# Value weights in their own buffers, and six weight residues made by accumulating DMAs, in a two-layer decoder trunk in float32

## The chip, the core and the metric

The kernel runs on one core of a Trainium2 chip. A core has a matrix engine (TensorE; the profile calls its matmuls PE and its weight loads PEld), a vector engine (VectorE, DVE), a scalar engine (ScalarE, ACT), a general engine (GpSimd, POOL) and an engine that mostly issues transfers (SyncE, SP). Transfers (DMAs) are issued on queues of SP, ACT and POOL; each engine works through its own list of instructions in order. The metric is the device time of one execution in microseconds.

## The reference

The input is one sequence of 256 tokens of width 1024. All weights and all arithmetic are float32.

```
h = x
hn = rms_norm(h, g[0,0])
h += stick_breaking_attention(hn, w_qkv, w_o)           # 16 heads of 64
h += (relu(rms_norm(h, g[0,1]) @ w1[0])**2) @ w2[0]     # 1024 -> 4096 -> 1024
shared = nsa_shared_kv(h, kv_norm, ...)                 # keys and values, compressed blocks
hn = rms_norm(h, g[1,0])
h += nsa_attention(hn, w_q, gate_b, w_o, shared)        # compressed, selected and window branch, gated
h += (relu(rms_norm(h, g[1,1]) @ w1[1])**2) @ w2[1]
out = rms_norm(h, final_norm)
```

In `stick_breaking_attention` the product `hn @ w_qkv` gives queries, keys and values. The kernel makes the values first.

## The kernel before

**Number format.** Matmuls run on the type fp32r, a float32 rounded to fewer bits. To keep float32's precision, each operand is split into a high part (a cast to fp32r, `wh` for weights) and a low part (what the cast lost, `wl = raw - wh`). A product is then made of three matmuls: high by high, high by low and low by high.

**The weight stream.** All weights come as one list of pieces (`stream`), most of 128 partitions by 2048 columns (1 MB), in the order of their use: the values' weights `wv` first, then `wqk`, `wo0`, the first MLP's `w1` and `w2` (alternating: `w1` piece c, then `w2` piece c-2), and so on. `fetch` (L252 to L265) issues the load of the next piece on SP into one of three buffers `raw`. `split` (L276 to L307) makes the two parts, half a piece at a time: the cast on ACT (L293), the subtraction on DVE (L299). After the second half's subtraction it calls `fetch` for the next piece, so a load waits until a buffer is read out. The parts lie in three buffers each (`wh`, `wl`, `NB = 3`); a piece can be split once TensorE is done with the piece three before it.

**The order of the work.** TensorE's instructions are in the order of the program. What ACT, DVE and POOL do, and in which order, is decided while the program is written out, by a planner (`Order`): it keeps a clock, a cost formula for each operation, a rank for each chain of operations and an expected landing time for each load (`ws.landed`), and gives each engine, when free, the ready operation of the lowest rank. Its choice is then fixed; at run time an engine that waits holds up all that stands behind it.

**The start** (`layer0`, from L555). Eight warming matmuls run until data come. The values `pv` are made from x, transposed, in blocks of 128 of its 1024 columns (k = 0 to 7). `load` brings the blocks of x (`xraw`; the first on ACT's queue, the others on SP's), `turned` splits a block into `xa` high (L568 on ACT or L569 on DVE) and low (L571). `v_first` computes block 0 with the first two weight pieces of 256 KB, `v_proj` the others with pieces cut by `V_CUT`: five of one block (512 KB) and one of two (1 MB). The residual stream `hres` and constants are loaded behind them, then the eight pieces `wqk`; `proj` makes queries and keys (`qk`). A broadcast of the norm's factor (`pr`) stands between values and queries.

**The first MLP** (`mlp`). For each of 16 column blocks c, `first` multiplies the activations by `w1` piece c (`pu`: for each half of 128 output columns, eight wide matmuls with the high weights, then eight narrow ones with the low weights), then `second` multiplies the squared result of block c-2 by a `w2` piece (`acc`).

**The end** (`finish`). For each token tile the squares are summed on ACT (L1431), the sum is closed on DVE (L1434), its power -0.5 is taken on POOL (L1436), the residual stream is multiplied by the gain on DVE (L1425), and the rows are scaled on ACT (L1418, 384 columns) and on DVE (L1420, two pieces of 320 columns); each scaled piece is stored at once (L1421).

Of the kernel before, what the change touches and what calls it, by code (L numbers as in the profile page):

```python
# [8 lines left out]
F32 = mybir.dt.float32  # L9
# [3 lines left out]
OP = mybir.AluOpType  # L13
AX = mybir.AxisListType

P = 128
D = 1024
T = 2
NK = D // P
NH = 16  # L20
DH = 64
# [3 lines left out]
DFF = 4096  # L25
NFC = 16
NGN = 6
V_CUT = ((1, 1), (2, 1), (3, 1), (4, 1), (5, 1), (6, 2))
EPS = 1e-5
NEG = -1e30  # L30
GELU_C = 2.0 * 0.7978845608028654
# [1 line left out]
C_CAP, C_ANY, C_COS, C_SIN, C_BLK, C_PW, C_ROT, C_ROS, C_CMT, C_CB, C_END = (  # L33
    0, 384, 386, 418, 450, 458, 462, 718, 974, 1230, 1486)
# [124 lines left out]
def act(n, f, more=0):  # L159
    return {"A": (195 + 0.835 * n + more, f, False)}  # L160
# [6 lines left out]
def pool(n, f, more=0):  # L167
    return {"G": (185 + 1.67 * n + more, f, True)}
# [3 lines left out]
def hybrid_kernel(ctx, tc, x, xt, eye, gcols, gfin, wqk, wv, wo0, wkv, wvs, wq, wg, wo1, w1, w2, cw1, cw2, cpos, gate_b, consts, out):  # L172
    nc = tc.nc

    cp = ctx.enter_context(tc.tile_pool(name="cp", bufs=1))
    wp = ctx.enter_context(tc.tile_pool(name="wp", bufs=3))
# [4 lines left out]
    o = Order()  # L181

    def go(gen, rank=1, lag=LAG):
        return Chain(o, gen, rank, o.now + lag)
# [6 lines left out]
    def slot(i, shape, dt, name):  # L191
        return cp.tile(shape, dt, tag=f"e{i}", name=name, bufs=1)
# [49 lines left out]
    i_m.append(feed_mlp(1))  # L242

    class Weights:
        raws, made, parts, gone, cur, landed = [], [], [], 0, -1, 0.0

    ws = Weights()
    ways = {"hi": "A"}

    def fetch():  # L250
        j = len(ws.raws)
        if j == len(stream):  # L252
            return
        src, n, whole = stream[j]
        raw = wp.tile([P, n], F32, tag="raw", name="raw", bufs=3)
        ws.raws.append(raw)
        ws.made.append(None)
        cuts = 2 if j == 0 else 1
        for c in range(cuts):
            r = slice(c * n // cuts, (c + 1) * n // cuts)  # L260
            nc.sync.dma_start(raw[:, r], src[:, r])
        for h in range(2):
            if h < cuts:
                ws.landed = max(o.t + 1900, ws.landed) + P * n * 4 / cuts / 330
            ws.parts.append(Chain(o, whole_part(j, h) if whole else split(j, h), rank_of(j), ws.landed))  # L265

    def rank_of(j):
# [7 lines left out]
    def split(j, half):  # L275
        n = stream[j][1]  # L276
        if 2 * j + half:
            yield ws.his[2 * j + half - 1]
        before = [i for i in range(j) if not stream[i][2]]
        while len(before) >= NB and ws.gone <= before[-NB]:  # L280
            w = Waiter()
            ws.waiting.append(w)
            yield w
        ws.parts[2 * j + half].rank = rank_of(j)
        r = slice(half * n // 2, (half + 1) * n // 2)

        def hi(e):
            def f():
                if ws.made[j] is None:
                    ws.made[j] = (wp.tile([P, n], F32R, tag="wh", name="wh", bufs=NB),  # L290
                                  wp.tile([P, n], F32R, tag="wl", name="wl", bufs=NB))
                if e == "A":
                    nc.scalar.copy(ws.made[j][0][:, r], ws.raws[j][:, r])  # L293
                else:
                    nc.vector.tensor_copy(ws.made[j][0][:, r], ws.raws[j][:, r])
            return f

        def lo():
            nc.vector.tensor_sub(ws.made[j][1][:, r], ws.raws[j][:, r], f32(ws.made[j][0][:, r]))  # L299

        m = n // 2
        k = {"A": (195 + 0.835 * m, hi("A"), False), "D": (200 + 0.49 * m, hi("D"), True)}
        yield {e: k[e] for e in ways["hi"]}
        ws.his[2 * j + half].finish()
        yield {"D": (150 + 1.045 * m, lo, True)}
        if half:
            fetch()  # L307

    class Waiter(Chain):
# [76 lines left out]
    def rstd_of(t, rs):  # L386
        v = []
        yield from variance(t, v)
        r = sp.tile([P, 1], F32, name="r", bufs=4)
        yield pool(1, lambda: nc.gpsimd.tensor_tensor(r, v[0], npow, op=OP.pow), 370)  # L390
        rs[t] = r
# [162 lines left out]
    def layer0(ap):  # L554
# [3 lines left out]
            mm(warm, nc.const_aps.tensor(1.0, [P, P], BF16), nc.const_aps.tensor(1.0, [P, 512], BF16), True, True)  # L558
        xn = x_tiles(0, "a")
        v = slot(0, [P, T, D], F32, "v0")  # L560
        xg = slot(1, [P, NK + NK * T * P], F32, "xraw")
        xraw = xg[:, NK:].rearrange("p (k q) -> p k q", k=NK)
        pv = [[B(2 * n + t, f"pv{t}{n}") for n in range(2)] for t in range(T)]
        in_x = [None] * NK

# [6 lines left out]
                xn[1][:, k, :], xraw[:, k, :], g, f32(xn[0][:, k, :]), op0=OP.mult, op1=OP.subtract), port=True)  # L572

        def load(k0, k1):
            a, b = NK * (k0 > 0) + k0 * T * P, NK + k1 * T * P
            (nc.sync if k0 else nc.scalar).dma_start(xg[:, a:b], xt[:, a:b])
            ws.landed = max(o.t + 1900, ws.landed) + P * (k1 - k0) * 1024 / 330
            for k in range(k0, k1):
                in_x[k] = Chain(o, turned(k), 0.4, ws.landed)

# [13 lines left out]
        def v_proj(i):  # L594
            k0, m = V_CUT[i]
            for kk in range(m):
                k = k0 + kk
                o.need(in_x[k])
                for n in range(2):
                    w = W(i_v[i], n if m == 1 else kk)  # L600
                    c = cut(w, kk * D + n * 512, kk * D + (n + 1) * 512)
                    for a, b in ((0, 0), (1, 0), (0, 1)):
                        for t in range(T):
                            mm(pv[t][n], tok(xn, k, t)[a], c[b], False, k == NK - 1 and b == 1)
            gone(i_v[i])
# [2 lines left out]
        o.run(o.now)  # L608
        load(0, 1)
        fetch()  # L610
        fetch()
        load(1, 2)
        fetch()
        load(2, 4)
        nc.scalar.dma_start(gc, gcols)
        go_on = ap.tile([P, 2 * ROW], BF16, name="go_on", bufs=1)
        nc.gpsimd.memset(go_on, 1.0)
        nc.gpsimd.memset(go_on.rearrange("p (h c) -> p h c", h=2)[:, :, 2 * SEG - 1:ROW:SEG], 0.0)
        v_first(0)
        v_first(1)  # L620
        load(4, 8)
        v_proj(0)
        v_proj(1)
        for t in range(T):
            nc.sync.dma_start(hres[t], x[t * P:(t + 1) * P, :])
        nc.sync.dma_start(ident, eye)
        nc.sync.dma_start(cst[:, 0:C_ROT], consts[:, 0:C_ROT])
        ws.landed = max(o.t + 1900, ws.landed) + 4500
        rstd = [None, None]
        rc = [Chain(o, rstd_of(t, rstd), 1.5, ws.landed) for t in range(T)]  # L630
        v_proj(2)
        v_proj(3)
        v_proj(4)
        v_proj(5)
        o.need(*rc)
        rbq = ap.tile([P, 2, T * P], F32, name="rbq", bufs=1)
        pr = B(6, "pr")
# [762 lines left out]
    nc.sync.dma_start(gf, gfin.to_broadcast([P, D]))  # L1400
    ssq = [sp.tile([P, 4], F32, name=f"ssq{t}", bufs=1) for t in range(T)]
    ys = [slot(1 + t, [P, 2, D], F32, f"ys{t}") for t in range(T)]
    last, gained = [[], []], [[], []]
    ends = [[(0, 512)]] * 3 + [[(0, 256), (256, 512)]]

    def finish(i, q, c):
        t, n = divmod(i, 2)
        k = len(last[t])
        end = i % 2 == 1 and q[1] == 512
        q = slice(n * 512 + q[0], n * 512 + q[1])  # L1410
        m = q.stop - q.start
        ss, sq, y = ssq[t], ys[t][:, 0, :], ys[t][:, 1, :]
        part = ss[:, 3:4]

        def scaled(e, a, b):
            def f():
                if e == "A":
                    nc.scalar.activation(y[:, a:b], y[:, a:b], AF.Copy, scale=part)  # L1418
                else:
                    nc.vector.tensor_scalar(y[:, a:b], y[:, a:b], part, None, op0=OP.mult)  # L1420
                (nc.scalar if e == "A" else nc.sync).dma_start(out[t * P:(t + 1) * P, a:b], y[:, a:b])  # L1421
            return {"A": (290 + 0.84 * (b - a), f, False)} if e == "A" else {"D": (200 + 0.49 * (b - a), f, True)}

        def gain():
            yield dve(m, lambda: nc.vector.scalar_tensor_tensor(  # L1425
                y[:, q], hres[t][:, q], float(D) ** 0.5, gf[:, q], op0=OP.mult, op1=OP.mult), port=True)

        def gen():
            yield c
            gained[t].append(go(gain(), 0.3, 0))  # L1430
            yield act(m, lambda: nc.scalar.activation(sq[:, q], hres[t][:, q], AF.Square, accum_out=ss[:, k:k + 1]), 190)  # L1431
            if k:
                yield last[t][k - 1]
            yield dve(1, lambda: nc.vector.tensor_scalar(part, ss[:, k:k + 1], part if k else D * EPS, None, op0=OP.add))  # L1434
            if end:
                yield pool(1, lambda: nc.gpsimd.tensor_tensor(part, part, npow, op=OP.pow), 370)  # L1436
                for g in gained[t]:
                    yield g
                yield [scaled("A", 640, 1024), scaled("D", 0, 320)]
                yield [scaled("D", 320, 640)]  # L1440

        last[t].append(go(gen(), 0.2))

# [36 lines left out]
def _layout(inp):  # L1480
# [3 lines left out]
    def cont(v):  # L1484
        return np.ascontiguousarray(v)

    def blocks(w, nk, cw):
# [11 lines left out]
    hg = (np.arange(3)[:, None] * NH + h[None, :]).reshape(-1)  # L1499
    f = {  # L1500
        "x": cont(a["x"][0]),
        "xt": cont(np.concatenate([a["norm_gain"].reshape(4, D)[0].reshape(NK, P).T, a["x"][0].T.reshape(NK, P, T * P).transpose(1, 0, 2).reshape(P, NK * T * P)], 1)),
        "eye": np.eye(P, dtype=np.float32),
        "gcols": cont(np.concatenate([a["norm_gain"].reshape(4, D), a["kv_norm"][None], a["final_norm"][None]], 0)
                      .reshape(NGN, NK, P).transpose(2, 0, 1).reshape(P, NGN * NK)),
# [36 lines left out]
```

## Time and profile before

| what | value |
|---|---|
| median of 2 runs | 623.19 us (623.17 to 623.21) |
| profiled execution | 623.1 us |
| its span | 621.0 us |
| mean granted clock of TensorE | 0.998 |
| HBM read | 106.61 MB, 173 GB/s over the span |
| DMA packets of SP's queue | 17280, 107.11 MB |

The profile shows one execution. The span runs from the first instruction to the last. Busy times are per engine. A row of the timeline has start, length, engine, line, operation, written tile, read tiles and shapes, and in brackets how long the engine stood idle before and what ended that. A row of the chain of work has start and length of a stretch of the chain that ended last, followed back from the last instruction. The groups of loads give size and median time from issue to landing. The rows themselves stand with the prediction, where they are used.

### The profile page before, as it was taken

What the parts mean: (1) busy time and instruction counts of PE and PEld (TensorE: products, weight loads), DVE (VectorE), ACT (ScalarE), POOL (GpSimd) and SP (SyncE); (2) the same over time, 40 slices, a digit from 0 to 9 for tenths busy, and PEclk for the clock granted to TensorE, in tenths of its full rate; (3) what the DMA queues carried; (4) which work ended last, traced back from release to release, by engine and by line L of the source; (5) the groups of instructions that cost most, each with busy time, mean ns of one, the idle gap of its engine ahead of it and who ended that gap; (6) DMA issues with size and microseconds to landing.
All of it is one profiled execution on the core that took longest, in us unless ns stands there. A gap on an engine that the chain in (4) does not pass through costs nothing.

```text
span 621.0 us, 8967 instructions
## 1 busy us (share of the span) xinstructions
PE 610.7 (98%) x3580; PEld 513.4 (83%) x3580; DVE 424.5 (68%) x615; ACT 328.3 (53%) x563; POOL 41.2 (7%) x57
## 2 busy tenths in 40 slices
PE   8999999999999999999999999999999999999995
PEld 5799997888888888888887788677888888888884
DVE  4688996686656666555938999873876665566655
ACT  4657675464555444543906776452654554444432
POOL 0000000000000000000111542310000000000000
PEclk9999999999999999999999999999999999999999
DMA  7974425255554545555355363112365555455501
GB/s 260 369 283 158 142 99 179 86 220 195 203 205 172 188 183 203 204 176 218 140 203 204 136 204 137 69 69 102 137 218 197 194 194 212 163 191 189 204 1 68
DMA packets 17898, 108.24 MB, mean 174 GB/s; under 512 B 2368, under 2 KB 4160, under 8 KB 5696
## 3 DMA queue, kind: packets, MB, share of 16 engines
q1 hardware_dynamic: 17280, 107.11, 47.5%
q8 instruction: 28, 0.46, 0.3%
q10 hardware_dynamic: 576, 0.55, 0.3%
q14 instruction: 14, 0.11, 0.0%
HBM read 106.61 MB, written 1.05 MB: 173 GB/s over the span
## 4 chain that ended last, share of the span: by engine, by line
PE 82%; DVE 10%; DMA 3%; ACT 2%; issue 2%; SPq 0%; POOLq 0%; POOL 0%; DVEq 0%; ACTq 0%
PE acc L347 34%; PE pu L347 29%; PE qk L347 7%; DVE wl L299 4%; PE pk L347 4%; PE po L347 3%; PE z L347 2%; DMA raw<-in_wqk 1%; DVE nm L1084 1%; PE qp L347 1%; PE pt L359 1%; PE pa L359 1%; PE ptp L359 1%; DMA raw<-in_wv 1%; DMA xraw<-in_xt 1%
## 5 line engine op out<-in xcount | busy, mean ns | idle before, releaser
L299 DVE TENSOR_TENSOR wl<-raw,wh 128x1024 fp32r<-128x1024 f32 (+2 forms) x196 | 227.8, 1185 | 110.1 <-ACT wh L293 110.0
L293 ACT CAST wh<-raw 128x1024 fp32r<-128x1024 f32 (+2 forms) x196 | 193.9, 1018 | 116.7 <-PE acc L347 46.3
L347 PE MATMUL pu<-xn,wh 128*128 128x512 f32 x512 | 130.7, 394 | 0.0
L347 PEld LDWEIGHTS pu<-xn,wh 128*128 128x128 f32 x512 | 93.3, 188 | 18.7 <-issue 0.5
L347 PE MATMUL acc<-wh,hh 128*128 128x512 f32 (+1 forms) x256 | 99.7, 389 | 0.0
L347 PE MATMUL acc<-wl,hh 128*128 128x512 f32 (+1 forms) x256 | 99.6, 389 | 0.0
L347 PE MATMUL acc<-wh,hl 128*128 128x512 f32 (+1 forms) x256 | 99.4, 388 | 0.0
L347 PEld LDWEIGHTS pu<-xn,wl 128*128 128x128 f32 x512 | 70.8, 189 | 6.1
L347 PE MATMUL pu<-xn,wl 128*128 128x256 f32 x512 | 72.4, 281 | 0.0
L347 PEld LDWEIGHTS acc<-wh,hl 128*128 128x128 f32 x256 | 48.0, 188 | 10.0
L347 PEld LDWEIGHTS acc<-wh,hh 128*128 128x128 f32 x256 | 48.1, 188 | 9.1
L347 PEld LDWEIGHTS acc<-wl,hh 128*128 128x128 f32 x256 | 48.2, 188 | 8.9
L513 ACT CAST hh<-ms 128x512 fp32r<-128x512 f32 x32 | 19.9, 622 | 61.3 <-DVE ms L512 61.3
L347 PE MATMUL qk<-xa,wh 128*128 128x256 f32 x256 | 46.8, 285 | 0.0
L347 PE MATMUL acc<-wh,oT 128*128 128x512 f32 x128 | 43.7, 404 | 0.7 <-DVE oT L437 0.7
L347 PEld LDWEIGHTS qk<-xa,wh 128*128 128x128 f32 x256 | 39.2, 189 | 0.5 <-issue 0.3
L347 PE MATMUL qk<-xa,wl 128*128 128x256 f32 x128 | 36.1, 282 | 0.6 <-DVE wl L299 0.6
L499 ACT COPY mr<-pu 128x256 f32<-128x256 f32 x64 | 23.6, 369 | 24.2 <-PE pu L347 24.2
L514 DVE TENSOR_TENSOR hl<-ms,hh 128x512 fp32r<-128x512 f32 x32 | 22.1, 692 | 19.4 <-ACT hh L513 19.4
L347 PE MATMUL pk<-wh,xk 128*128 128x512 f32 (+1 forms) x128 | 33.6, 342 | 0.0
L1078 ACT ACTIVATE pe<-z,nm 128x256 f32<-128x256 f32 (+1 forms) x64 | 26.1, 428 | 12.7 <-DVE nm L1084 12.6
L347 PEld LDWEIGHTS acc<-wh,oT 128*128 128x128 f32 x128 | 24.0, 188 | 6.7 <-DVE oT L437 0.9
(178 smaller groups left out, 731.7 us busy)
## 6 DMA issues: line engine op xcount, KB each, us to landing
raw<-in_w SPq DMA_DIRECT2D x64, 1024.0 KB, 4.8
raw<-in_wqk SPq DMA_DIRECT2D x8, 1024.0 KB, 5.6
raw<-in_wo SPq DMA_DIRECT2D x8, 1024.0 KB, 4.8
raw<-in_wkv SPq DMA_DIRECT2D x4, 1024.0 KB, 4.9
raw<-in_cw SPq DMA_DIRECT2D x4, 1024.0 KB, 4.8
raw<-in_wq SPq DMA_DIRECT2D x4, 1024.0 KB, 4.9
raw<-in_wv SPq DMA_DIRECT2D x5, 512.0 KB, 5.0
raw<-in_wvs SPq DMA_DIRECT2D x2, 1024.0 KB, 5.0
```

The source lines that it names most:

```text
L293: nc.scalar.copy(ws.made[j][0][:, r], ws.raws[j][:, r])
L299: nc.vector.tensor_sub(ws.made[j][1][:, r], ws.raws[j][:, r], f32(ws.made[j][0][:, r]))
L347: nc.tensor.matmul(o_, a, b, start=first, stop=last, skip_group_check=True)
L359: nc.tensor.transpose(o_, a, i)
L499: yield act(256, lambda: nc.scalar.copy(r[:, q], pu[f][:, 256:512]))
L513: yield act(512, lambda: nc.scalar.copy(hh, sv))
L514: yield dve(512, lambda: nc.vector.tensor_sub(hl, sv, f32(hh)), port=True)
L1078: return act(n, lambda: nc.scalar.activation(d, z, AF.Exp, bias=nm[:, i:i + 1], accum_out=rs[:, t, hd, b:b + 1]), 150)
L1084: yield dve(256 * (t + 1), lambda: nc.vector.tensor_reduce(nm[:, i:i + 2], z, axis=AX.X, op=OP.max, negate=True))
```

## The change

1. The value weights' pieces get a buffer each (`rv`, in a pool of the first layer) in place of the three shared ones, and `V_CUT` has three pieces of one block and two of two blocks. Some pieces are loaded in two halves. All loads of the values, of x, of `hres` and of the constants, and the first three `wqk` pieces, are issued one after another at the start; `split` calls `fetch` only behind the value weights. Block 1 of x goes on ACT's queue; the gain columns ahead of x are padded from 8 to 64 columns.
2. The planner's landing times come from a new formula (`lands`).
3. For `w1` pieces 3, 5, 7, 9, 11 and 13 of the first MLP, the low part is made in another way: ACT writes minus the high part (`raw` times -1, rounded) into `wl`, and a DMA issued by POOL adds `raw` to it, in place. The planner books 5000 ns for it.
4. At the end the last gain multiplication is issued behind the sum's closing, and the rows are scaled in one piece of 704 columns on DVE and one of 320 on ACT.

```diff
-V_CUT = ((1, 1), (2, 1), (3, 1), (4, 1), (5, 1), (6, 2))
+V_CUT = ((1, 1), (2, 1), (3, 1), (4, 2), (6, 2))
...
+    def lands(n):
+        ws.path = max(ws.path, o.t + 1100)
+        ws.path += n / (270 if ws.path < 10000 else 390)
+        ws.landed = ws.path + 1300
...
-        raw = wp.tile([P, n], F32, tag="raw", name="raw", bufs=3)
+        if j in i_v0 or j in i_v:
+            raw = ws.pool.tile([P, n], F32, name=f"rv{j}", bufs=1)
+        else:
+            raw = wp.tile([P, n], F32, tag="raw", name="raw", bufs=3)
...
-        cuts = 2 if j == 0 else 1
+        cuts = 2 if j in (0, 2) or j in i_v[-2:] else 1
...
-        yield {"D": (150 + 1.045 * m, lo, True)}
-        if half:
+        if j in i_m[0][0][3:15:2]:
+            low = ws.made[j][1][:, r]
+            yield act(m, lambda: nc.scalar.mul(low, ws.raws[j][:, r], -1.0))
+            nc.gpsimd.dma_start(f32(low), ws.raws[j][:, r], accum_op=OP.add)
+            w = Waiter()
+            o.at(o.t + 5000, w.finish)
+            yield w
+        else:
+            yield {"D": (150 + 1.045 * m, lo, True)}
+        if half and j > i_v[-1]:
             fetch()
...
-            (nc.sync if k0 else nc.scalar).dma_start(xg[:, a:b], xt[:, a:b])
+            (nc.sync if k0 > 1 else nc.scalar).dma_start(xg[:, a:b], xt[:, a:b])
...
         load(0, 1)
         fetch()
-        fetch()
         load(1, 2)
         fetch()
+        fetch()
         load(2, 4)
-        nc.scalar.dma_start(gc, gcols)
+        fetch()
+        fetch()
+        load(4, 6)
+        fetch()
+        load(6, 8)
+        fetch()
+        nc.sync.dma_start(gc, gcols)
...
+        for _ in range(3):
+            fetch()
...
-                yield [scaled("A", 640, 1024), scaled("D", 0, 320)]
-                yield [scaled("D", 320, 640)]
+                yield [scaled("A", 704, 1024), scaled("D", 0, 704)]
```

SP's queue at the start, before: each load of `wv` from the third on goes into a buffer `raw` that has to be read out first.

```order
L261 DMA raw<-in_wv 128x256 x2
L261 DMA raw<-in_wv 128x512
L576 DMA xraw<-in_xt 128x256
L261 DMA raw<-in_wv 128x1024
L576 DMA xraw<-in_xt 128x512
L261 DMA raw<-in_wv 128x1024 x2
L576 DMA xraw<-in_xt 128x1024
L261 DMA raw<-in_wv 128x1024 x2
L261 DMA raw<-in_wv 128x2048
```

The same place with the change (`rv` are the buffers of their own):

```order
L269 DMA rv_97<-in_wv 128x256 x2
L269 DMA rv_101<-in_wv 128x512
L269 DMA rv_103<-in_wv 128x512 x2
L593 DMA xraw<-in_xt 128x512
L269 DMA rv_107<-in_wv 128x1024
L269 DMA rv_109<-in_wv 128x1024
L593 DMA xraw<-in_xt 128x512
L269 DMA rv_112<-in_wv 128x1024 x2
L593 DMA xraw<-in_xt 128x512
L269 DMA rv_116<-in_wv 128x1024 x2
```

Block 1 of x (128 x 256) is gone from this queue, and each row has a target that nothing read before. On DVE at the start, before:

```order
L569 TENSOR_SCALAR xa<-xraw 128x256
L571 SCALAR_TENSOR_TENSOR xa<-xraw,xa 128x256
L299 TENSOR_TENSOR wl<-raw,wh 128x256 x2
L569 TENSOR_SCALAR xa<-xraw 128x256
L299 TENSOR_TENSOR wl<-raw,wh 128x256
```

and with the change:

```order
L586 TENSOR_SCALAR xa<-xraw 128x256
L588 SCALAR_TENSOR_TENSOR xa<-xraw,xa 128x256
L307 TENSOR_TENSOR wl<-rv_97,wh 128x256 x2
L588 SCALAR_TENSOR_TENSOR xa<-xraw,xa 128x256
L307 TENSOR_TENSOR wl<-rv_101,wh 128x256 x2
```

The high part of block 1 (second TENSOR_SCALAR) has left DVE; ACT makes it, behind its first two casts and ahead of the next two. ACT in the first MLP, around the split of a `w1` piece, before:

```order
L293 CAST wh_1659<-raw_1550 128x1024
L513 CAST hh_1657<-ms_1607 128x512
L293 CAST wh_1701<-raw_1592 128x1024 x2
L499 COPY mr_1698<-pu0_1696 128x256
L293 CAST wh_1745<-raw_1647 128x1024
```

and with the change:

```order
L301 CAST wh_1659<-raw_1590 128x1024
L529 CAST hh_1657<-ms_1607 128x512
L301 CAST wh_1701<-raw_1593 128x1024 x2
L315 ACTIVATE wl_1702<-raw_1593 128x1024
L515 COPY mr_1698<-pu0_1696 128x256
L315 ACTIVATE wl_1702<-raw_1593 128x1024
L301 CAST wh_1745<-raw_1647 128x1024
```

The two negations stand behind the piece's two casts, on either side of the copy; the two subtractions of that piece are gone from DVE, and two DMAs stand on POOL.

More of the change, by code (lines that the diff above doesn't have):

```diff
@@ L244, in hybrid_kernel @@
     class Weights:
-        raws, made, parts, gone, cur, landed = [], [], [], 0, -1, 0.0
+        raws, made, parts, gone, cur, landed, path, pool = [], [], [], 0, -1, 0.0, 0.0, None
     ws = Weights()
     ways = {"hi": "A"}
+    def lands(n):
+        ws.path = max(ws.path, o.t + 1100)
+        ws.path += n / (270 if ws.path < 10000 else 390)
+        ws.landed = ws.path + 1300
     def fetch():
@@ L263, in fetch @@
             if h < cuts:
-                ws.landed = max(o.t + 1900, ws.landed) + P * n * 4 / cuts / 330
+                lands(P * n * 4 // cuts)
             ws.parts.append(Chain(o, whole_part(j, h) if whole else split(j, h), rank_of(j), ws.landed))
@@ L560, in layer0 @@
         v = slot(0, [P, T, D], F32, "v0")
-        xg = slot(1, [P, NK + NK * T * P], F32, "xraw")
-        xraw = xg[:, NK:].rearrange("p (k q) -> p k q", k=NK)
+        ws.pool = ap
+        xg = slot(1, [P, DH + NK * T * P], F32, "xraw")
+        xraw = xg[:, DH:].rearrange("p (k q) -> p k q", k=NK)
         pv = [[B(2 * n + t, f"pv{t}{n}") for n in range(2)] for t in range(T)]
@@ L574, in load @@
         def load(k0, k1):
-            a, b = NK * (k0 > 0) + k0 * T * P, NK + k1 * T * P
-            (nc.sync if k0 else nc.scalar).dma_start(xg[:, a:b], xt[:, a:b])
-            ws.landed = max(o.t + 1900, ws.landed) + P * (k1 - k0) * 1024 / 330
+            a, b = DH * (k0 > 0) + k0 * T * P, DH + k1 * T * P
+            (nc.sync if k0 > 1 else nc.scalar).dma_start(xg[:, a:b], xt[:, a:b])
+            lands(P * (k1 - k0) * 1024)
             for k in range(k0, k1):
@@ L610, in layer0 @@
         fetch()
-        fetch()
         load(1, 2)
         fetch()
+        fetch()
         load(2, 4)
-        nc.scalar.dma_start(gc, gcols)
+        fetch()
[5 more added lines that the diff above has]
+        nc.sync.dma_start(gc, gcols)
+        for t in range(T):
+            nc.sync.dma_start(hres[t], x[t * P:(t + 1) * P, :])
+        nc.sync.dma_start(ident, eye)
+        nc.sync.dma_start(cst[:, 0:C_ROT], consts[:, 0:C_ROT])
+        lands(1250000)
+        rstd = [None, None]
+        rc = [Chain(o, rstd_of(t, rstd), 1.5, ws.landed) for t in range(T)]
+        for _ in range(3):
+            fetch()
         go_on = ap.tile([P, 2 * ROW], BF16, name="go_on", bufs=1)
@@ L620, in layer0 @@
         v_first(1)
-        load(4, 8)
         v_proj(0)
         v_proj(1)
[L624 to L630, printed above, removed]
         v_proj(2)
@@ L633, in layer0 @@
         v_proj(4)
-        v_proj(5)
         o.need(*rc)
@@ L1402, in hybrid_kernel @@
     ys = [slot(1 + t, [P, 2, D], F32, f"ys{t}") for t in range(T)]
-    last, gained = [[], []], [[], []]
+    last, gained, late = [[], []], [[], []], [[], []]
     ends = [[(0, 512)]] * 3 + [[(0, 256), (256, 512)]]
@@ L1429, in gen @@
             yield c
-            gained[t].append(go(gain(), 0.3, 0))
+            late[t].append(gain)
+            if not end:
+                gained[t].append(go(late[t].pop()(), 0.3, 0))
             yield act(m, lambda: nc.scalar.activation(sq[:, q], hres[t][:, q], AF.Square, accum_out=ss[:, k:k + 1]), 190)
@@ L1435, in gen @@
             if end:
+                gained[t].extend(go(g(), 0.2, 0) for g in late[t])
                 yield pool(1, lambda: nc.gpsimd.tensor_tensor(part, part, npow, op=OP.pow), 370)
@@ L1501, in _layout @@
         "x": cont(a["x"][0]),
-        "xt": cont(np.concatenate([a["norm_gain"].reshape(4, D)[0].reshape(NK, P).T, a["x"][0].T.reshape(NK, P, T * P).transpose(1, 0, 2).reshape(P, NK * T * P)], 1)),
+        "xt": cont(np.concatenate([a["norm_gain"].reshape(4, D)[0].reshape(NK, P).T, np.zeros((P, DH - NK), np.float32), a["x"][0].T.reshape(NK, P, T * P).transpose(1, 0, 2).reshape(P, NK * T * P)], 1)),
         "eye": np.eye(P, dtype=np.float32),
```

## The prediction

> **What bounds the kernel now.** The page's first part and its chain of work come first. Of the 621.0 us of the span TensorE is busy for 610.7, and 82% of the chain is matmuls.
>
> ```profile
> PE 610.7 (98%) x3580; PEld 513.4 (83%) x3580; DVE 424.5 (68%) x615; ACT 328.3 (53%) x563; POOL 41.2 (7%) x57
> PE 82%; DVE 10%; DMA 3%; ACT 2%; issue 2%; SPq 0%; POOLq 0%; POOL 0%; DVEq 0%; ACTq 0%
> ```
>
> Matmul ends are modelled, so this share alone could hide waits. The sums by stretch show the stages: start, opening of the value projection, end of it, the first MLP, the second layer's attention, the end. Columns: stretch, length, then busy time and count for PE, PEld, DVE, ACT, POOL, then granted clock, DMA share, GB/s.
>
> ```profile
> 0.00:5.50 5.50, 4.69 (x15) 2.11 (x16) 1.51 (x4) 2.30 (x4) 1.10 (x7) 1.00 0.59 157
> 5.50:8.50 3.00, 1.75 (x9) 0.99 (x7) 1.42 (x4) 0.67 (x3) 0.00 (x0) 1.00 0.98 374
> 20.00:30.00 10.00, 9.56 (x45) 7.62 (x43) 3.84 (x7) 6.34 (x9) 1.23 (x5) 1.00 1.03 422
> 134.00:279.00 145.00, 145.00 (x737) 123.18 (x736) 88.84 (x110) 71.35 (x98) 0.00 (x0) 1.00 0.53 192
> 327.00:394.00 67.00, 66.07 (x521) 52.58 (x519) 63.22 (x117) 44.31 (x127) 26.62 (x19) 1.00 0.47 166
> ```
>
> In the first MLP (134 to 279) TensorE never pauses, DVE is at 61%, ACT at 49%, the DMA at half, and POOL does nothing. A DVE operation taken out there saves no time. Room is left at the start (1.75 of 3.00 us busy from 5.5 to 8.5) and in the second attention (327 to 394), where DVE, at 94%, sets the pace and where the change issues nothing of its own. The granted clock is 1.00 in all five rows, so it explains nothing here.
>
> **The start, step by step.** Rows of the timeline; in brackets, idle time before and its releaser.
>
> ```profile
> 2.11 0.43 SPq L576 DMA_DIRECT2D xraw<-in_xt  x1
> 2.59 0.43 SPq L261 DMA_DIRECT2D raw<-in_wv  x1
> 3.67 0.40 ACT L293 CAST wh<-raw 128x256 fp32r<-128x256 f32 x1 [1.65 <-DMA raw<-in_wv]
> 5.29 0.72 ACT L293 CAST wh<-raw 128x256 fp32r<-128x256 f32 x2 [0.56 <-DMA raw<-in_wv]
> 7.06 0.35 DVE L569 TENSOR_SCALAR xa<-xraw 128x256 fp32r<-128x256 f32 x1 [1.63 <-DMA xraw<-in_xt]
> 8.06 0.42 DVE L299 TENSOR_TENSOR wl<-raw,wh 128x256 fp32r<-128x256 f32 x1
> 8.34 1.15 ACT L293 CAST wh<-raw 128x512 fp32r<-128x512 f32 x2 [2.33 <-DMA raw<-in_wv]
> 8.53 0.73 PE L347 MATMUL pv<-wl,xa 128*128 128x512 f32 x2 [1.28 <-DVE wl L299]
> 9.11 1.11 PE L347 MATMUL pv<-wh,xa 128*128 128x512 f32 x4
> 28.25 0.62 PE L347 MATMUL pv<-wl,xa 128*128 128x512 f32 x2
> ```
>
> TensorE idles 1.28 us at 8.53. It waits for a low part that DVE, in order, holds behind the split of block 1 of x; that block, issued at 2.11, came at 7.06. From 9.11 to the end near 28.5 it runs with no wait of that size, 84 wide matmuls in 19.4 us, 0.23 each. So only the time at which block 1's matmuls begin (9.0) counts.
>
> After the change block 1 leaves on ACT's queue behind block 0, about 0.9 us sooner, and DVE no longer stands behind its first step, since its high part goes to ACT. I work the landings out from the rows. The piece of 256 KB cast at 5.29 now has 32 KB of padding and block 1's 128 KB beside it; at 157 GB/s that is up to 1.0 us, so its casts end at 6.01 + 0.8 = 6.8 (I take 0.8, since the two queues share). Its four high matmuls then end near 7.75, its two low ones at 8.2. The 512 KB piece of block 1, cast from 8.34, is issued 0.48 us earlier (2.59 becomes 2.1) and in halves: the first half lacks 262 KB at 374 GB/s, 0.7 us, hence lands near 7.2 and, cast in 0.58, is ready at 7.8; the second at 8.5, when the first half's matmuls still run. Block 1 begins at 8.2: **minus 0.8 us**. Bounds: minus 1.3 (the whole wait of 1.28 gone) and plus 0.6: if block 1 still came at 7.06, ACT, whose new order puts its step ahead of the casts (0.5 us, then 0.72), would release the four high matmuls only at 8.3, and block 1 would begin at 9.6.
>
> The Trainium skill bears on this (DMA: Bandwidth & Descriptors, "Issuing engines are not separate DMA queues"): transfers of all issuing engines share the same DMA engines and interleave, and a second issuer saves only issue time. By it block 1 lands no sooner, this term is the plus 0.6 just bounded, and the sum below would be 623.0. The 0.98 busy share of the row from 5.5 to 8.5 agrees with full engines; the 0.59 before it does not.
>
> The next wait is at the first query/key piece, in the chain:
>
> ```profile
> 18.92 8.73 DMA raw<-in_wqk
> 27.75 1.05 ACT wh L293
> 28.83 1.24 DVE wl L299
> 30.11 14.23 PE qk L347 x118
> 30.11 0.39 PE L347 MATMUL qk<-xa,wl 128*128 128x256 f32 x1 [0.55 <-DVE wl L299]
> ```
>
> Its load waited for a buffer until 18.92 and landed at 27.65 behind the residual stream. With value weights in buffers of their own, all loads up to this one are issued in 20 steps of 0.43 us, by 10 us. Ahead of this piece and with it lie 4.2 MB of value weights, 2.2 of x in both layouts, 0.3 of constants and 1.05 of its own, 7.7 MB: 0.9 by 5.5 us, the rest at 374 to 422 GB/s, done by 24. Cast and low part take 2 x 1.05 and 1.24 us more: 27.3, against the use near 28.5 less 0.8 plus 0.8 for the broadcast's matmuls, 28.5. The wait goes, 0.55 by its row and 0.7 if matmuls are counted by starts: **minus 0.7 us**. TensorE then runs on without a wait of this size to 327, so the shift lasts. Loads early on cost nothing more: what they fill stood idle (0.59 busy).
>
> **The accumulating DMAs.** Six pieces, w1 pieces 3, 5, ... 13 of the first MLP, each in two halves: 12 DVE subtractions leave, 12 ACT multiplications and 12 DMAs of 512 KB from POOL come. Piece 5 stands for all:
>
> ```profile
> 151.03 5.62 PE pu L347 x32
> 156.65 5.45 PE acc L347 x24
> 162.10 5.62 PE pu L347 x32
> 151.11 2.00 ACT L293 CAST wh<-raw 128x1024 fp32r<-128x1024 f32 x2 [1.32 <-PE acc L347]
> 153.87 0.37 ACT L499 COPY mr<-pu 128x256 f32<-128x256 f32 x1 [0.76 <-PE pu L347]
> 152.19 2.36 DVE L299 TENSOR_TENSOR wl<-raw,wh 128x1024 fp32r<-128x1024 f32 x2 [1.68 <-ACT wh L293]
> 166.85 1.05 ACT L293 CAST wh<-raw 128x1024 fp32r<-128x1024 f32 x1 [1.36 <-issue]
> raw<-in_w SPq DMA_DIRECT2D x64, 1024.0 KB, 4.8
> ```
>
> Its buffers come free at 151.03, and its matmuls start at 162.10. Eight wide high matmuls go first, two thirds of 2.81 us, so the low part's first half is due at 164.0 and the second at 164.4. ACT negates at 153.1 to 154.2 and, after the copy, at 154.5 to 155.5 (a cast of this shape takes 1.05). DMA one may start at 154.3, DMA two at 155.6. No accumulating DMA is in the trace. Lower bound of a half: the plain rate, 0.52 MB at the 422 GB/s of the row from 20 to 30, 1.2 us (the 1 MB load moves 1.05 MB in 2.5 of its 4.8 us, so 2.3 are fixed). Upper bound: both inputs read at the slowest pace seen, 1.05 MB at 157 GB/s, 6.7 us. Nearest is the 1 MB load, which also moves 1.05 MB: 2.5 us of transfer. So both halves are in by 154.3 + 2.3 + 5.0 = 161.6, **2.8 us ahead of need: 0**. Cover: the two pieces ahead (5.62 + 5.45 us). It is gone if a half takes over 3.9 us, (164.4 - 154.3 - 2.3) / 2; each us above costs 2 us a piece, 12 us in all.
>
> Queued behind: on POOL nothing until the attention. On SP the load three pieces on now waits for the accumulation to finish reading its buffer, 161.6 in place of 154.5; it lands at 166.4, for a cast at 166.85 of a piece that TensorE wants 11 us later. Later loads queue behind it in the half of the DMA time that is free. ACT gains 12 x 1.05 us over 130, from 49% to about 57%: hidden under matmuls, like the 14.4 us that DVE loses.
>
> The skill (SBUF — State Buffer, "Who interferes with whom") says that a DMA of GpSimd's can be held while DVE runs copies or scalings in a two-port mode, and that two-input operations take the reading port alone. DVE's frequent rows here are of the second kind, so by it nothing is held: 0 as well. Were the issue held through the pair of 2.36 us, the limit would sink from 3.9 to 2.7 us a half; that is the rule that speaks against this part, and it raises the first rival's chance below.
>
> **The end.** TensorE stops at 614.3; then the chain runs alone.
>
> ```profile
> 614.02 0.28 PE L347 MATMUL accz<-wh,hl 128*128 128x256 f32 x1
> 615.13 0.75 DVE L1425 SCALAR_TENSOR_TENSOR ys<-hres,gf 128x256 f32<-128x256 f32 x2
> 615.45 0.19 ACT L1431 ACTIVATION_READ_ACCUMULATOR ys<-hres 128x1 f32 x1
> 615.79 0.21 DVE L1434 TENSOR_SCALAR ssq<-ssq 128x1 f32<-128x1 f32 x1
> 616.66 0.68 DVE L1420 TENSOR_SCALAR ys<-ys,ssq 128x320 f32<-128x320 f32 x2 [0.66 <-POOL ssq L1436]
> out<-ys SPq DMA_DIRECT2D x4, 160.0 KB, 1.9
> ```
>
> The sum of squares no longer stands behind the gain: 0.1 us. One scaling of 704 columns (about 0.56: 0.34 and 384 more columns at 0.5 ns or so) replaces two ending after 0.68: 0.1. The last store starts some 0.4 us earlier with its issue, but is 352 KB in place of 160, 0.46 us more at 422 GB/s. **0**, between minus 0.3 and plus 0.3.
>
> **The second attention** has the same matmuls in the same order, but the planner's clock differs, and DVE, ACT and POOL interleave otherwise: one copy goes from DVE to ACT, one multiply each way between DVE and POOL. DVE loses some 0.6 us there; a swapped pair can make TensorE wait for one weight subtraction (1.24). I take **0**, between minus 1.5 and plus 1.5.
>
> **Sum.** 623.1 us for the profiled execution (span 621.0 and 2.1 around it; the runs' median, 623.19, is the same) less 0.8 and 0.7: **621.6 us**.
>
> **Rivals.** *Slow accumulation.* Past 3.9 us a half TensorE waits for low parts at six places. At the upper bound of 6.7 us it is 2 x 2.8 us a piece, 34 in all: 655; from 5.1 us a half (plus 14.4 less 1.5) it is slower by over 2%. For it: no row shows a DMA that reads two inputs, and the limit is only 1.6 times my value. Against: during the accumulation SP is held, so the DMA is nearly free. *No gain at the start.* Block 1 lands as late as before, the 0.6 is lost and 0.7 won: 623.0. For it: before, 0.8 MB was on its way ahead of 7.06, and as much is now. Against: the gap between 0.59 and 0.98 busy. *The attention's new interleaving* outweighs the rest: 620.1 to 623.1, inside the range.
>
> **Chances.** My forecast 0.64, no gain at the start 0.18, the attention's interleaving 0.07, slow accumulation 0.11, of which 0.09 ends over 2% slower and the rest a few us up. **Range** 619.0 to 626.0: all gains at their best are 1.3 + 0.7 + 0.3 + 1.5 = 3.8, so 619.3; upward it takes in the first three cases and an accumulation up to 0.4 us a half past the limit, and leaves out about 0.1. A measurement of this kernel can tell about 2% (12.5 us) from no change. Faster by more 0.02, within 0.89, slower 0.09.
>
> **What would show it.** Right: block 1's high matmuls at about 8.2, query/key matmuls from 27.7 on without a wait for low parts, TensorE busy through the whole first MLP, accumulating DMAs landing within 8 us of issue. Wrong: waits of TensorE for the low parts at each second w1 piece; ACT waiting for block 1 of x beyond 6 us; loads landing so late that casts wait for them in the MLP.

## The result, and the profile after

The changed kernel takes 619.45 us (median of 2 runs, 619.44 to 619.46) against 623.19 us: the ratio is 0.9931, 95% interval 0.9912 to 0.9951. The prediction was 621.6 us, 619.0 to 626.0. The time lies in the range, and less than 2% apart from before, but the gain is 3.7 us where 1.5 was forecast. The profiled execution is one of the two runs (619.44 us, span 617.7). The parts of its page that answer to those shown of before, busy times and the chain of work:

```profile
PE 609.4 (99%) x3580; PEld 515.1 (83%) x3580; DVE 408.3 (66%) x597; ACT 340.7 (55%) x575; POOL 51.4 (8%) x69
PE 95%; DMA 2%; ACT 1%; issue 1%; DVE 1%; POOL 0%; SPq 0%; POOLq 0%; DVEq 0%; ACTq 0%
```

DVE has left the chain (10% before, 1% now), and matmuls are 95% of it. Yet TensorE's busy time also fell, from 610.7 to 609.4, with the same 3580 matmuls. So a part of the gain is not a wait that went; the matmuls themselves follow each other faster.

The start, rows of the timeline:

```profile
4.62 0.51 ACT L585 ACTIVATE xa<-xraw 128x256 fp32r<-128x256 f32 x1
5.82 1.99 ACT L301 CAST wh<-rv 128x256 fp32r<-128x256 f32 x4 [0.69 <-DMA rv<-in_wv]
6.58 1.19 PE L363 MATMUL pv<-wh,xa 128*128 128x512 f32 x4
8.08 1.08 PE L363 MATMUL pv<-wh,xa 128*128 128x512 f32 x4
```

Block 1 of x is split at 4.62, and its high matmuls begin at 8.08 (9.11 before). Its load, before and after (size, us from issue to landing):

```profile
xraw<-in_xt SPq DMA_DIRECT2D x1, 128.0 KB, 4.9
xraw<-in_xt ACTq DMA_DIRECT2D x1, 128.0 KB, 3.3
```

Issued at 2.11 it landed at 7.0; issued at 1.19 it lands at 4.5. The weight piece of 256 KB, which is ahead of it in both kernels, did not gain: it is cast at 5.82, before at 5.29. The chain from there to the queries and keys:

```profile
1.65 4.15 DMA rv<-in_wv
6.58 20.71 PE pv L363 x90
27.29 0.44 PE pr L363 x4
```

No load, cast or subtraction stands between the values and the query/key matmuls any more.

The first MLP: the chain around the piece that stood for all in the prediction, then POOL's issues for it, the group of the accumulating DMAs, and the sum over 111 to 276.

```profile
148.98 5.56 PE pu L363 x32
154.54 5.47 PE acc L363 x24
160.01 5.08 PE pu L363 x28
```

```profile
152.32 0.87 POOL L316 DMA_DIRECT2D wl<-raw  x1 [19.19 <-ACT mr L515]
153.59 0.89 POOL L316 DMA_DIRECT2D wl<-raw  x1 [0.41 <-ACT wl L315]
```

```profile
wl<-raw POOLq DMA_DIRECT2D x12, 512.0 KB, 5.2
```

```profile
111.00:276.00 165.00, 165.00 (x855) 141.43 (x854) 91.88 (x123) 95.57 (x132) 10.65 (x12) 1.00 0.70 225
```

TensorE is busy for all of the 165.00 us. The issues of POOL end 0.87 to 0.89 us after they begin, and the halves land a median of 5.2 us after them; this piece's landed at 156.94 and 159.63, and its matmuls began at 160.01. Before, a `pu` block of 32 matmuls took 5.62 us in the chain, now 5.56.

The end, rows of the timeline and the group of stores:

```profile
610.46 0.28 PE L363 MATMUL accz<-wh,hl 128*128 128x256 f32 x1
613.09 0.56 ACT L1441 ACTIVATE ys<-ys,ssq 128x320 f32<-128x320 f32 x1 [1.02 <-POOL ssq L1462]
613.09 0.58 DVE L1443 TENSOR_SCALAR ys<-ys,ssq 128x704 f32<-128x704 f32 x1 [0.44 <-POOL ssq L1462]
```

```profile
out<-ys SPq DMA_DIRECT2D x2, 352.0 KB, 2.7
out<-ys ACTq DMA_DIRECT2D x2, 160.0 KB, 2.4
```

From the last matmul's start to the end of the span it is 617.66 - 610.46 = 7.20 us, before 6.98. The store that lands last is ACT's of 160 KB: the group's median is 2.4 us, this one took 2.89. The same first matmuls of each stage, marked in both traces, give the whole account (us from the span's start):

| mark | before | after | gain in the stage |
|---|---|---|---|
| block 1's first high matmul | 9.11 | 8.08 | 1.03 |
| the broadcast `pr`, behind the values | 28.71 | 27.13 | 0.55 |
| first `qk` matmul with a low part | 30.11 | 27.81 | 0.72 |
| first `pu` of the first MLP | 116.61 | 114.66 | -0.35 |
| its last `pu` | 278.18 | 275.55 | 0.68 |
| first `ph`, behind the shared keys | 319.19 | 316.66 | -0.10 |
| first `pu` of the second MLP | 436.13 | 432.54 | 1.06 |
| last matmul | 614.02 | 610.46 | -0.03 |
| end of the span | 621.00 | 617.66 | -0.22 |
| profiled time | 623.10 | 619.44 | 0.32 |

Start and lost wait are 1.03 + 0.72 = 1.75, near the forecast of 1.5. Three rows are new: 0.55 in the values, 0.68 in the first MLP, 1.06 in the second attention.

### The profile page after: what moved, and what is told of

Read it like the earlier page. It is cut to its first block, busy times and chain, and to the rows that moved or that the text cites. A ratio compares the mean times of both kernels' runs of the same rounds, so it can differ in the third digit from the quotient of the medians.

```text
span 617.7 us, 9006 instructions
## 1 busy us (share of the span) xinstructions
PE 609.4 (99%) x3580; PEld 515.1 (83%) x3580; DVE 408.3 (66%) x597; ACT 340.7 (55%) x575; POOL 51.4 (8%) x69
## 4 chain that ended last, share of the span: by engine, by line
PE 95%; DMA 2%; ACT 1%; issue 1%; DVE 1%; POOL 0%; SPq 0%; POOLq 0%; DVEq 0%; ACTq 0%
PE acc L363 35%; PE pu L363 29%; PE qk L363 8%; PE pk L363 5%; PE pv L363 3%; PE po L363 3%; PE z L363 3%; PE qp L363 3%; PE ptp L375 2%; DMA raw<-in_wq 1%; PE ph L363 1%; PE pt L375 1%; PE pa L375 1%; DMA rv<-in_wv 1%; ACT pe L1101 0%
## 5 line engine op out<-in xcount | busy, mean ns | idle before, releaser
L307 DVE TENSOR_TENSOR wl<-raw,wh 128x1024 fp32r<-128x1024 f32 x168 | 202.0, 1222 | 100.3 <-ACT wh L301 100.3
L301 ACT CAST wh<-raw 128x1024 fp32r<-128x1024 f32 x180 | 184.8, 1053 | 103.1 <-PE acc L363 44.5
L516 DVE TENSOR_TENSOR mu<-pu,mr 128x256 f32<-128x256 f32 x64 | 26.6, 418 | 20.8 <-ACT mr L515 20.8
```

Of the source, the lines that this page charges most:

```text
L516: yield dve(256, lambda: nc.vector.tensor_add(u[:, q], pu[f][:, 0:256], r[:, q]))
```

## The experiments

Each experiment's ratio is against runs of the kernel before made with it, whose medians are 623.46 to 623.86 us, so medians of different experiments compare to some tenths of a microsecond.

In the stages where the matmuls come closer, their starts are 227 to 229 ns apart after the change, for matmuls of 512 columns, and 233 before; those of 256 columns are 119 to 120 apart after it and 117 to 118 before. In `acc` blocks and in the second MLP nothing differs. My theory: SBUF addresses. The padding of the gain columns makes the buffer of x 8448 bytes a partition in place of 8224, so all that is allocated behind it moves: by the program's addresses the split weights stood 32 bytes off the x operand, modulo 256, and now stand at 0. Rivals: the accumulating DMAs, which free DVE, gave the pace or the attention's gain; the attention's gain comes from the addresses too; or from the planner's new landing times, which change DVE's order there.

**A gap of 32 bytes in the kernel before, behind x and ahead of x.** The first moves the weights against x, the second moves both.

```diff
         xg = slot(1, [P, NK + NK * T * P], F32, "xraw")
+        gap = cp.tile([P, 8], F32, name="gap")
```

```diff
+        gap = cp.tile([P, 8], F32, name="gap")
         xn = x_tiles(0, "a")
```

> The kernel before with 32 bytes per partition left empty behind the buffer of x, nothing else: every engine's order is the same, only addresses from there on move, so that the tile of x, the split weights and all other tiles stand at 32 bytes past a multiple of 64, as in the changed kernel. Theory 'phase' (a matmul of 512 columns takes 233 ns where its stationary and its moving operand differ in their address modulo 64 bytes, and 227 where they agree; one of 256 columns 117 and 120): wide matmuls of the value projection and of the first MLP's first product fall from 233 to 227 ns, narrow ones of the query/key projection rise from 118 to 120; 622.3 to 622.7 us. If the gain of 1.0 us in the second attention is also of the addresses, 621.3 to 621.7. Rival 'the pace has to do with the loads or with DVE traffic, which the change moved': 623.2 us, paces as before.

> The kernel before with the same 32 bytes left empty ahead of the tile of x: now that tile stands at a multiple of 64 and the split weights, the second tile of x and the rest at 32 past one. Theory 'phase': operands of the value projection and the first MLP's first product still differ, so 233 and 117 ns stay there and the time is 623.2 us. Rival 'a tile at 32 past a multiple of 64 is itself slow': the first MLP falls to 227 ns and the second MLP, whose operands now both stand at 32 past, rises to 233: its 16 blocks become 0.6 us longer.

Behind x: 621.04 us, 0.9961 (0.9946 to 0.9976). Ahead of x: 623.92 us, 1.0006 (0.9997 to 1.0016), and the old paces of 233 and 117. So an unused gap of 32 bytes moves the time, and what counts is the distance of the two operands, not the address of one. But the first form of the theory, a rule modulo 64, fell: the distance of 64 gave 114 for the narrow matmuls and left the wide ones at 233, not at 227.

**The same gap in the changed kernel, and the change without its accumulating DMAs.** The first puts the distance back to 32 and keeps the rest. The second makes all low parts on DVE again.

```diff
         xg = slot(1, [P, DH + NK * T * P], F32, "xraw")
+        gap = cp.tile([P, 8], F32, name="gap")
```

```diff
-        if j in i_m[0][0][3:15:2]:
+        if j in ():
```

> The changed kernel with 32 bytes left empty behind the buffer of x, so that the addresses modulo 64 are those of the kernel before; all orders are those of the changed kernel. Theory 'phase': wide matmuls of the value projection and the first MLP go back to 233 ns, and 619.45 rises by 0.5 to 1.0 us. The second attention keeps its gain of 1.0 us if that comes of the order of DVE, ACT and POOL, and loses it if it comes of the addresses (then 621.0 to 621.5). Rival: 619.45, paces as in the changed kernel.

> The changed kernel without the accumulating DMAs: all low parts are subtracted on DVE again; start, end and addresses are the change's. Theory 'hidden': the first MLP takes the same 11.03 us per block, and the total differs from 619.45 only by what another interleaving does to the second attention (up to 1.0 us either way). Rival 'the accumulation frees DVE and so makes the first MLP faster': the first MLP gets 0.5 us or more longer.

With the gap: 620.35 us, 0.9951 (0.9935 to 0.9968). The paces are the old ones: the first MLP's `pu` blocks span 161.57 us again, as before the change (160.89 after it), and the values behind block 1's first high matmul take 19.69 us (19.61 before, 19.05 after). But the second attention still takes 115.92 us (116.94 before, 115.88 after). So the pace hangs on the addresses, and the attention's gain of 1.06 us does not. Without accumulation: 619.62 us, 0.9937 (0.9923 to 0.9952), first MLP 160.89 and attention 115.86, as with it. The accumulating DMAs are worth nothing here, either way.

**Gaps of 64, 128 and 192 bytes in the changed kernel** (16, 32 and 48 in place of the 8 above).

> The changed kernel with 64 bytes left empty behind the buffer of x; orders as in the changed kernel. The runs so far fit a pace that depends on how far apart the two operands stand modulo 256 bytes: 0 apart gives 227 ns (512 columns) and 120 (256 columns), 32 apart 233 and 117, 64 apart 233 and 114. Theory 'distance': the value projection goes to 233 ns (plus 0.5 us), the 384 narrow matmuls of the query/key projection to 114 ns (minus 2.3 us), the first MLP stays at 11.03 us per block; 617.2 to 617.9 us. Rival 'the 114 ns of the one run came of its longer stalls in loading': paces of 0 apart, 619.45 us.

> The changed kernel with 128 bytes left empty there: operands 128 apart modulo 256. If the pace depends on the distance modulo 256, narrow matmuls take 114 ns or less and wide ones about 233, and the time is 617.0 to 618.0 us; if it depends on the distance modulo 128, paces are those of 0 apart (227 and 120 ns) and the time is 619.4 us.

> The changed kernel with 192 bytes left empty, so that the split weights stand 64 bytes short of the tile of x modulo 256, in place of 64 past it. If only the size of the distance modulo 256 counts, narrow matmuls of the query/key projection take 114 ns and the time is near 617.2 us. If its direction counts too, they take more; 618.5 to 620.5 us.

64: 617.16 us, 0.9899 (0.9884 to 0.9914). 128: 620.23 us, 0.995 (0.9935 to 0.9964). 192: 618.97 us in its one run. The chain's rows for the first query/key matmuls, 120 of 256 columns, after the change and with gaps of 64, 128 and 192, in this order:

```profile
27.73 14.39 PE qk L363 x120
```

```profile
28.49 13.62 PE qk L363 x120
```

```profile
28.59 14.40 PE qk L363 x120
```

```profile
27.90 14.13 PE qk L363 x120
```

The same matmuls take from 13.62 to 14.40 us. Distances between the starts, in ns:

| distance, bytes modulo 256 | `pu` of the first MLP, 512 columns | the same, 256 columns |
|---|---|---|
| 0 (changed kernel) | 229 | 119 |
| 32 (before; change with gap 32) | 233 | 118 |
| 64 (gap 64; before with gap behind) | 233 | 114 |
| 128 | 232 | 119 |
| 192 | 231 | 118 |

Distance 64 is best for this kernel, since queries and keys are made of narrow matmuls alone: from the first low `qk` matmul to the first MLP it takes 85.08 us in place of 86.85. (The interval of this run and that of the changed kernel just touch; the stretch of the trace does not depend on the start.) The second attention is shorter too, 115.31 us in place of 115.88 (116.48 in place of 116.94 with the gap behind x in the kernel before), so it is not free of the addresses either. 64 and 192 differ, so the direction counts too. With 64 the expectation failed for the values, whose wide matmuls went to 228 to 230 ns and not to 233; so the distance alone does not give the pace. With 128 neither branch of the expectation held fully: the wide matmuls were not fast, nor the narrow ones. No rule that foretells the five rows was found.

**Block 1 of x on SP's queue.**

```diff
-            (nc.sync if k0 > 1 else nc.scalar).dma_start(xg[:, a:b], xt[:, a:b])
+            (nc.sync if k0 else nc.scalar).dma_start(xg[:, a:b], xt[:, a:b])
```

> The changed kernel with block 1 of x loaded on SP's queue, between the second and the third piece of the value weights, as before the change; ACT's and DVE's orders are the change's. Theory 'ACT's queue brings block 1 early, and with it the start' (the prediction's term of minus 0.8 us and its bound of plus 0.6): block 1 lands at 6.5 to 7.1 us, ACT waits for it ahead of the casts, and block 1's matmuls begin at 9.4 to 9.7 us in place of 8.1: 620.6 to 621.1 us. Rival 'queues interleave anyway' (the skill's rule): same landing on either queue, 619.4 us.

620.99 us, 0.9961 (0.9948 to 0.9973); its runs spread from 620.47 to 622.81, and the profiled one is the longest. Its start:

```profile
5.22 0.51 ACT L585 ACTIVATE xa<-xraw 128x256 fp32r<-128x256 f32 x1 [0.78 <-DMA xraw<-in_xt]
7.64 1.88 ACT L301 CAST wh<-rv 128x256 fp32r<-128x256 f32 x4 [1.91 <-DMA rv<-in_wv]
8.40 1.65 PE L363 MATMUL pv<-wh,xa 128*128 128x512 f32 x3 [2.18 <-ACT wh L301]
```

The expectation says that this brings back the old order, but it does not: here block 1 is issued at 1.65, ahead of the second weight piece of 256 KB, where before the change it stood behind that piece. Block 1 is there by 5.22; on ACT's queue it was there by 4.62, when ACT came to it. What comes late, in this run, is the weight piece that now stands behind it on SP: cast at 7.64 in place of 5.82, with TensorE idle for 2.18 us while block 1 lies ready. The size was about as expected and the mechanism was not: a block ahead of the weight piece delays that piece. This says nothing of the change's own gain, since in neither of the two kernels does block 1 stand ahead of it. For that gain the traces speak: block 1 landed at 4.3 to 4.7 us in all nine runs that load it on ACT's queue, and at 6.2 to 7.5 in the four with the loads of before. How much of it is the queue and how much the earlier issue, no run separates. The median's loss of 1.5 us against the changed kernel is uncertain, since the two intervals touch.

**Each accumulating DMA twice.** A second one adds a tile of zeros, so the output stays.

```diff
             nc.gpsimd.dma_start(f32(low), ws.raws[j][:, r], accum_op=OP.add)
+            nc.gpsimd.dma_start(f32(low), ws.zero, accum_op=OP.add)
...
+            ws.zero = ap.tile([P, 1024], F32, name="zero", bufs=1)
+            nc.gpsimd.memset(ws.zero, 0.0)
```

> The changed kernel with a second accumulating DMA behind each of the twelve, which adds a tile of zeros (512 KB) to the same low part once the first has landed. The output stays the same. In the changed kernel piece 5's second half landed at 159.63 us and was due at about 162.3. Theory of the prediction (a limit past which TensorE waits): the second half now lands some 9 to 10 us later, 6 to 8 us past its need, at six pieces: 36 to 48 us more, 655 to 667 us. Rival 'the low parts have far more slack than was worked out, through buffers or the order of the matmuls': under 625 us.

739.25 us in its one run, far above the expectation. The chain around the first piece, and the group of the narrow `pu` matmuls (busy, mean ns, idle before them):

```profile
130.75 4.67 DMA wl<-raw
...
147.66 10.60 DMA wl<-zero
```

```profile
L364 PE MATMUL pu<-xn,wl 128*128 128x256 f32 x512 | 81.7, 301 | 101.5 <-DMA wl<-zero 101.5
```

TensorE waits 101.5 us for the second DMAs, 17 a piece; the rest of the 120 us is slower matmuls (those of `pu` are busy for 17.5 us more, at a mean granted clock of 0.921 in place of 0.996). Only the first of a piece's four DMAs is as fast as in the changed kernel, 4.67 us here. The next two, which overlap, take 8.81 and 10.80 beside one load of 1 MB; the last takes 10.60 beside two such loads, which were held until 147.32, when the piece's buffer had been read. So there is a limit past which TensorE waits, as the prediction said. That the accumulation stays fast in the changed kernel because SP's load must wait for it fits these rows, but no run shows it by itself.

**The landing formula alone, both ways**: the kernel before with the new formula, and the changed kernel with the old one.

```diff
+    def lands(n):
+        ws.path = max(ws.path, o.t + 1100)
+        ws.path += n / (270 if ws.path < 10000 else 390)
+        ws.landed = ws.path + 1300
...
-                ws.landed = max(o.t + 1900, ws.landed) + P * n * 4 / cuts / 330
+                lands(P * n * 4 // cuts)
...
```

```diff
     def lands(n):
-        ws.path = max(ws.path, o.t + 1100)
-        ws.path += n / (270 if ws.path < 10000 else 390)
-        ws.landed = ws.path + 1300
+        ws.landed = max(o.t + 1900, ws.landed) + n / 330
```

> The kernel before with the planner's new landing formula alone; its orders of DVE, ACT and POOL in the second attention become other ones (near those of the changed kernel), the loads, buffers, addresses and the end stay. From the first matmul with the combined compression weights to the first of the second MLP the kernel before took 116.94 us and the changed one 115.88. Theory 'the planner's times set the attention's order, and the order the 1.05 us': 115.8 to 116.2 us here, and 622.0 to 622.6 us in all if the start is unhurt. Rival 'the earlier loads or the freed DVE did it': 116.9 us, 623.2.

> The changed kernel with the old landing formula in the planner; loads, buffers, accumulating DMAs, addresses and the end are the change's, while DVE's order in the second attention is again that of the kernel before, row for row. Theory 'order': the stretch takes 116.9 us again, and the total rises by about 1 us to 620.3 to 620.7 if the start is unhurt. Rival: 115.9 us, 619.4.

Before with the new formula: 622.30 us, 0.9974 (0.9964 to 0.9985), and the second attention takes 115.93 us. The change with the old one: 620.41 us, 0.9952 (0.9935 to 0.9969), and it takes 116.80. The profiled run of the first also lost 1.8 us at the start, so its total says less than the stretch. The attention's gain goes with the formula, that is with the order of the engines' work. Where it arises on DVE, the chain of the kernel before and its wait show:

```profile
387.74 3.30 DVE wl L299 x2
391.04 0.60 DVE oT L437
```

```profile
PE acc L347 <- DVE oT L437: 0.7, 1, 0.7
```

DVE makes two halves of a weight's low part one after the other, and the attention's output `oT`, for which TensorE waits, stands behind both. DVE's timeline at that place after the change:

```profile
383.38 1.21 DVE L307 TENSOR_TENSOR wl<-raw,wh 128x1024 fp32r<-128x1024 f32 x1
384.52 0.72 DVE L1061 STREAM_SHUFFLE qw<-qu 128x512 f32<-128x512 f32 x1
385.14 1.20 DVE L307 TENSOR_TENSOR wl<-raw,wh 128x1024 fp32r<-128x1024 f32 x1
386.53 0.69 DVE L453 TENSOR_TENSOR oT<-po,oT 128x512 fp32r<-128x512 f32 x1 [0.19 <-ACT oT L452]
```

One half now goes ahead of the shuffle, and `oT` starts after an idle time of 0.19, as soon as ACT's part is there. With the old formula in the changed kernel the old row is back, and the wait with it:

```profile
385.02 3.42 DVE L305 TENSOR_TENSOR wl<-raw,wh 128x1024 fp32r<-128x1024 f32 x2
388.36 0.68 DVE L451 TENSOR_TENSOR oT<-po,oT 128x512 fp32r<-128x512 f32 x1
```

```profile
PE acc L361 <- DVE oT L451: 0.7, 1, 0.7
```

Matched matmul by matmul, the new order loses up to 1.0 us between 338 and 349 and then wins 2.0 back, most of it around this `oT`.

**Best of both**: the gap of 64, and the end scaled in three pieces again.

```diff
+        gap = cp.tile([P, 16], F32, name="gap")
...
-                yield [scaled("A", 704, 1024), scaled("D", 0, 704)]
+                yield [scaled("A", 640, 1024), scaled("D", 0, 320)]
+                yield [scaled("D", 320, 640)]
```

> The changed kernel with 64 bytes left empty behind the buffer of x (617.16 us in its own run) and, at the end, the two pieces of 320 columns on DVE and 384 on ACT of the kernel before, with the gain multiplication still behind the sum's closing. From the start of the last matmul to the span's end the kernel before took 6.98 us and the changed one 7.20. Theory 'the store of 352 KB, 2.7 us to landing against 1.9, costs 0.3 us and the later gain saves 0.1': 6.85 to 6.95 us, 616.8 to 617.0 in all. Rival: 7.2 us, 617.2.

616.95 us, 0.9889 (0.9873 to 0.9906): it beats both kernels. From the last matmul to the end it is 6.78 us, against 7.20 in the changed kernel and 6.98 before. Against the gap alone the medians differ by 0.2 us and the intervals overlap, so the end's part rests on that stretch of the trace.

## Where the prediction was right, and where it failed

The forecast gain was 1.5 us, and 3.7 came. Two steps of the sum failed. The second attention was put at 0, where the planner's new order was worth 1.06 us. And the padding of the gain columns had no term, where the addresses that it moves were worth about 0.9. The terms one by one:

- **Block 1 of x, minus 0.8.** Measured 1.03, with block 1 at 8.08 where 8.2 was worked out (and 9.11 before, where the sum used 9.0). The reason held: block 1 landed 2.6 us sooner, DVE no longer waits for it, and the wait of 1.28 us is gone. The Trainium skill (DMA: Bandwidth & Descriptors, "Issuing engines are not separate DMA queues") says that transfers of all issuers share the DMA engines; the rival that the prediction took from it, 623.0, did not come, so the rule alone does not foretell the start here: block 1 was issued 0.92 us sooner and landed 2.6 us sooner.
- **The query/key wait, minus 0.7.** Measured 0.72; the wait for the low part is gone. The first piece of `wqk` was issued at 14.27 and not by 10, since SP's issues came slower than one in 0.43 us, but it landed at 22.8, ahead of the 24 worked out. No run takes the buffers away by themselves; the stage takes 0.68 or 0.69 us in all ten runs with the change's loads, and 1.36 to 2.78 in the four with the loads of before.
- **Accumulating DMAs, 0.** Right, and shown by the run without them. The second half of piece 5 landed 7.3 us after ACT's first negation allowed the first issue, 159.63 - 152.32, as forecast (161.6 - 154.3). TensorE never waited for them. In the prediction the price of a half was 2.5 us of transfer and 2.3 fixed, together 4.8; the median is 5.2, midway between two kinds, 4.6 to 4.7 for the first half of a piece and 5.7 to 7.4 for the second, which starts beside the first. The Trainium skill's rule (SBUF — State Buffer, "Who interferes with whom") that two-input operations of DVE hold no issue of POOL's agrees with the trace: eleven of the twelve issues took 0.86 to 0.89 us, whether or not DVE ran such an operation beside them; the first took 1.03.
- **The end, 0 within 0.3.** Measured plus 0.22. The scaling ended sooner as forecast, and the last store was issued 0.26 us sooner after the last matmul (0.4 was forecast). It took 0.50 us longer to land, 2.89 in place of 2.39, near the 0.46 of the prediction; but it is ACT's store of 160 KB beside the larger one, which landed 0.19 us ahead of it.
- **The second attention, 0 within 1.5.** Here the sum was mis-sized: measured minus 1.06. The prediction named the mechanism, a swap of neighbours that makes TensorE wait for one weight subtraction, but only as something that the new order could bring. It did bring a loss, of up to 1.0 us. But the kernel before already had such a wait, at `oT`, and the new order took it away, most of the 2.0 us that it won back. The row of the wait, 0.7 us at 391, could be read in the trace of before.
- **A missing term, about minus 0.9** (0.55 - 0.35 + 0.68): the pace of the matmuls, by the distance of their operands in SBUF. The prediction counted the padding from 8 to 64 columns as 32 KB more to load, and gave the addresses that it moves no term. The changed kernel with a gap of 32 bytes, which puts the distance back, shows that it was this: the values and the first MLP take 0.64 and 0.68 us longer again, queries and keys 0.46 less.
- Around the span lie 1.8 us in place of 2.1, another 0.3 that no run explains.

The rivals fell as the prediction weighed them: no slow accumulation, and a gain at the start. The third, the attention's new interleaving, came on the good side with 1.06 of its 1.5 us, beside the start and not in place of it.

## What to carry to other kernels

When a diff changes the size of a buffer, look at what is allocated behind it: where TensorE has no waits left, a gap of 64 bytes was worth 2.3 us of 619 here, and it takes one run to try. When a planner's clock changes, look in the old trace for waits that a swap could take away as well as for those that it could bring. Work taken off an engine that nobody waits for is worth nothing, however much of it there is: 12 subtractions and 14.4 us of DVE here.

## What the runs showed of the hardware

- The distance between the starts of matmuls depends on where the two operands stand in SBUF against each other: 227 to 233 ns for 512 columns and 114 to 120 for 256, as in the rows above. Why, and what the rule is, stays open; five distances were tried.
- An accumulating DMA of 512 KB within SBUF took 4.62 us with no load beside it (the first half of piece 5), and 10.60 us beside two loads of 1 MB. Issuing it kept POOL for 0.86 to 0.89 us in eleven of twelve cases, with a two-input operation of DVE beside a part of it or none.
- The start's landings differ from run to run by some tenths of a microsecond and more: in the nine runs that load x and the first weights alike, the second weight piece landed between 5.2 and 6.4 us. With the gap of 64 TensorE waited 0.9 us there for a cast, which that edit does not explain.
